# A 2x2 average pool on one core: the scheduler's straight-line program, and hand-written hardware loops with semaphores that are counted back down

## The chip, the cores and the metric

One NeuronCore of one Trainium2 chip. The metric is the device time of one execution in microseconds (us), on that core. A profile comes from one execution; its "span" is about 1.8 us shorter than the time reported for the same execution (3102.3 and 3104.08 in the profile of the kernel before).

## The reference

```python
def setup_inputs():
    return {'x': np.random.randn(32, 128, 256, 256).astype(np.float32), 'kernel_size': 2, 'stride': 2}

def reference(x, kernel_size, stride):            # cut to what matters
    for i in range(h_out):
        for j in range(w_out):
            window = x[:, :, 2*i:2*i + 2, 2*j:2*j + 2]
            output[:, :, i, j] = np.mean(window, axis=(2, 3))
    return output                                  # (32, 128, 128, 128) float32
```

1073.7 MB are read and 268.4 MB written, for three additions and one multiplication per output. Moving the data is what takes the time: the profile below has the DMA engines 90% or more busy in every slice.

## The kernel before

A row pair of the image (512 values) gives one output row (128 values). A tile is 32 row pairs on each of 128 partitions: 8 MB in, 2 MB out. There are 127 whole tiles, and a last one that is loaded in four parts of 16, 8, 4 and 4 row pairs, so that the work after the last byte is short.

```python
    in_pool = ctx.enter_context(tc.tile_pool(name="inp", bufs=2))
    out_pool = ctx.enter_context(tc.tile_pool(name="outp", bufs=4))

    def pool(it, dst):
        nc.vector.tensor_add(out=it[:, :, 0:w], in0=it[:, :, 0:w], in1=it[:, :, w:])     # L54
        nc.vector.tensor_add(out=dst, in0=it[:, :, 0:w:2], in1=it[:, :, 1:w:2])          # L55
        nc.scalar.mul(out=dst, in_=dst, mul=0.25)                                        # L56
    # ... cut: block() gives the rows of a tile in x and in out, tiles() a pair of buffers
    for k in range(whole):                       # 127 tiles
        xt, ot = block(k * TILE * P, TILE)
        it, res = tiles()
        nc.sync.dma_start(out=it, in_=xt)
        pool(it, res)
        if k < whole - 1:
            nc.scalar.dma_start(out=ot, in_=res)
        else:
            held = (ot, res)                     # stored later, from SyncE
    # ... cut: the last tile's four loads, the held store, then for each part:
        pool(it[:, a:b], res[:, a:b])
        nc.scalar.dma_start(out=ot, in_=res[:, a:b])
```

The Python loop is written out into the program: the trace has 392 instructions on VectorE, 397 on ScalarE and 270 on SyncE. The framework (Tile) places every wait.

Of the kernel before, what the change touches and what calls it, by code (L numbers as in the profile page):

```python
# [1 line left out]

# [4 lines left out]


@with_exitstack  # L10
def kernel(
    ctx: ExitStack,
    tc: tile.TileContext,
    x: bass.AP,
    kernel_size: bass.AP,
    stride: bass.AP,
    out: bass.AP,
):
    nc = tc.nc
    P = nc.NUM_PARTITIONS  # L20

    n, c, h, w = x.shape
    k = int(kernel_size)
    s = int(stride)
    h_out = (h - k) // s + 1
    w_out = (w - k) // s + 1
    R = n * c * h_out
    units = R // P if R % P == 0 else 0


    if k == 2 and s == 2 and h % 2 == 0 and w == 256 and units >= 1024:
        _pool_2x2(ctx, tc, x, out, units)
    else:
        _generic_pool(ctx, tc, x, out, k, s, n, c, h, w, h_out, w_out)


TILE = 32


def _pool_2x2(ctx, tc, x, out, units):  # L40
    nc = tc.nc
    P = nc.NUM_PARTITIONS
    f32 = mybir.dt.float32
    w = x.shape[3]
    w_out = w // 2

    xv = x.rearrange("n c (ho a) w -> (n c ho) (a w)", a=2)
    ov = out.rearrange("n c ho wo -> (n c ho) wo")

    in_pool = ctx.enter_context(tc.tile_pool(name="inp", bufs=2))  # L50
    out_pool = ctx.enter_context(tc.tile_pool(name="outp", bufs=4))

    def pool(it, dst):
        nc.vector.tensor_add(out=it[:, :, 0:w], in0=it[:, :, 0:w], in1=it[:, :, w:])  # L54
        nc.vector.tensor_add(out=dst, in0=it[:, :, 0:w:2], in1=it[:, :, 1:w:2])  # L55
        nc.scalar.mul(out=dst, in_=dst, mul=0.25)  # L56

    def block(r0, g):
        rows = slice(r0, r0 + g * P)
        xt = xv[rows].rearrange("(p g) f -> p g f", p=P)  # L60
        return xt, ov[rows].rearrange("(p g) f -> p g f", p=P)

    def tiles():
        it = in_pool.tile([P, TILE, 2 * w], f32, name="in_tile")
        return it, out_pool.tile([P, TILE, w_out], f32, name="res")



    whole, rest = divmod(units - 1, TILE)
    rest += 1  # L70
    for k in range(whole):
        xt, ot = block(k * TILE * P, TILE)
        it, res = tiles()
        nc.sync.dma_start(out=it, in_=xt)  # L74
        pool(it, res)
        if k < whole - 1:
            nc.scalar.dma_start(out=ot, in_=res)
        else:
            held = (ot, res)



    it, res = tiles()
    parts, a = [], 0
    while a < rest:
        b = rest if rest - a <= 4 else a + (rest - a) // 2
        xt, ot = block((whole * TILE + a) * P, b - a)
        nc.sync.dma_start(out=it[:, a:b], in_=xt)
        parts.append((ot, a, b))
        a = b  # L90
    nc.sync.dma_start(out=held[0], in_=held[1])
    for ot, a, b in parts:
        pool(it[:, a:b], res[:, a:b])
        nc.scalar.dma_start(out=ot, in_=res[:, a:b])


def _generic_pool(ctx, tc, x, out, k, s, n, c, h, w, h_out, w_out):
    nc = tc.nc
    P = nc.NUM_PARTITIONS

    planes = n * c
    xp = x.rearrange("n c h w -> (n c) h w")
    op = out.rearrange("n c ho wo -> (n c) ho wo")

    if h_out <= 0 or w_out <= 0 or planes == 0:
        return

    max_in_bytes_per_part = 48 * 1024

    def rows_for(bi):  # L110
        return (bi - 1) * s + k

    BI = 1
    while BI < h_out and rows_for(BI + 1) * w * 4 <= max_in_bytes_per_part:
        BI += 1

    inv = 1.0 / float(k * k)

    pool = ctx.enter_context(tc.tile_pool(name="gen", bufs=2))

    for p0 in range(0, planes, P):
        pn = min(P, planes - p0)
        for i0 in range(0, h_out, BI):
            bi = min(BI, h_out - i0)
            rows_needed = rows_for(bi)

            in_t = pool.tile([P, rows_for(BI), w], mybir.dt.float32, name="g_in")
            nc.sync.dma_start(
                out=in_t[:pn, :rows_needed, :],
                in_=xp[p0 : p0 + pn, i0 * s : i0 * s + rows_needed, :],  # L130
            )

            acc = pool.tile([P, BI, w_out], mybir.dt.float32, name="g_acc")
            first = True
            for di in range(k):
                for dj in range(k):
                    src = in_t[
                        :pn,
                        di : di + (bi - 1) * s + 1 : s,
                        dj : dj + (w_out - 1) * s + 1 : s,  # L140
                    ]
                    if first:
                        nc.vector.tensor_copy(out=acc[:pn, :bi, :], in_=src)
                        first = False
                    else:
                        nc.vector.tensor_add(
                            out=acc[:pn, :bi, :], in0=acc[:pn, :bi, :], in1=src
                        )

            nc.scalar.mul(out=acc[:pn, :bi, :], in_=acc[:pn, :bi, :], mul=inv)  # L150

            nc.scalar.dma_start(
                out=op[p0 : p0 + pn, i0 : i0 + bi, :], in_=acc[:pn, :bi, :]
            )


# [1 line left out]
_INS = ['x', 'kernel_size', 'stride']  # L158
_OUTS = [((32, 128, 128, 128), 'float32')]

_NUMBERS = {'kernel_size': 2, 'stride': 2}


# [26 lines left out]
```

## Time and profile before

3104.2 us, median of 3 runs (3104.09 to 3104.42).

| | kernel before |
|---|---|
| DMA engines busy | 90% or more in all 40 slices |
| moved | 1342.26 MB, 433 GB/s over the span |
| VectorE busy | 54% |
| ScalarE busy | 15% |
| period of a tile | 24.18 us, of which VectorE works 13.2 |

The page of the kernel before. First the busy time of an engine; then the DMA's busy tenths and GB/s in 40 equal slices; then the DMA queues with packets, MB and share of the 16 engines; then groups of instructions (busy us, mean ns, idle us before them and what ended it).

```profile
span 3102.3 us, 1081 instructions
...
DVE 1679.7 (54%) x262; ACT 464.8 (15%) x132; POOL 0.2 (0%) x4
...
DMA  9999999999999999999999999999999999999999
GB/s 418 437 439 425 437 439 424 438 438 425 438 437 425 439 436 426 439 434 428 440 433 429 439 432 431 438 431 433 437 428 437 437 428 436 437 428 436 437 428 410
...
q1 hardware_dynamic: 19008, 1075.85, 80.1%
q10 hardware_dynamic: 18720, 266.35, 20.1%
q14 instruction: 8, 0.07, 0.0%
...
L54 DVE TENSOR_TENSOR in_tile<-in_tile 128x8192 f32<-128x8192 f32 (+1 forms) x131 | 1113.0, 8496 | 1404.2 <-DMA in_tile<-in_x_dram 1404.2
...
L55 DVE TENSOR_TENSOR res<-in_tile 128x4096 f32<-128x4096 f32 (+1 forms) x131 | 567.0, 4328 | 11.8 <-DVE in_tile L54 0.5
```

The DMA engines hardly rest: they are 90% or more busy in every slice, and loads (q1, 80.1%) and stores (q10, 20.1%) together fill them, at 433 GB/s. VectorE waits 1404 us in all, for loads. The small queue q14, of the kind "instruction" on the page, has 8 packets.

VectorE's timeline of the kernel before (start us, us long, what, idle before and what ended it):

```profile
22.69 8.69 DVE L54 TENSOR_TENSOR in_tile<-in_tile 128x8192 f32<-128x8192 f32 x1 [22.69 <-DMA in_tile<-in_x_dram]
...
42.02 8.69 DVE L54 TENSOR_TENSOR in_tile<-in_tile 128x8192 f32<-128x8192 f32 x1 [6.18 <-DMA in_tile<-in_x_dram]
...
66.57 8.69 DVE L54 TENSOR_TENSOR in_tile<-in_tile 128x8192 f32<-128x8192 f32 x1 [11.40 <-DMA in_tile<-in_x_dram]
...
477.66 8.69 DVE L54 TENSOR_TENSOR in_tile<-in_tile 128x8192 f32<-128x8192 f32 x1 [10.98 <-DMA in_tile<-in_x_dram]
...
501.84 8.69 DVE L54 TENSOR_TENSOR in_tile<-in_tile 128x8192 f32<-128x8192 f32 x1 [10.97 <-DMA in_tile<-in_x_dram]
510.62 4.43 DVE L55 TENSOR_TENSOR res<-in_tile 128x4096 f32<-128x4096 f32 x1
526.44 8.69 DVE L54 TENSOR_TENSOR in_tile<-in_tile 128x8192 f32<-128x8192 f32 x1 [11.39 <-DMA in_tile<-in_x_dram]
...
550.83 8.69 DVE L54 TENSOR_TENSOR in_tile<-in_tile 128x8192 f32<-128x8192 f32 x1 [10.77 <-DMA in_tile<-in_x_dram]
...
3067.22 8.69 DVE L54 TENSOR_TENSOR in_tile<-in_tile 128x8192 f32<-128x8192 f32 x1 [10.96 <-DMA in_tile<-in_x_dram]
```

Subtract the starts. From the third tile on the period is 24.18 us (477.66 to 501.84), but from 501.84 to 526.44 it is 24.60 and then 24.39. The trace's packet records put 8-KB packets of q14 at 525.3 and 540.4 us, in just this stretch. The last line is the last full load.

The tail of the kernel before, from its timeline (four of the parts' instructions and the issue of the last store):

```profile
3081.76 4.42 DVE L54 TENSOR_TENSOR in_tile<-in_tile 128x4096 f32<-128x4096 f32 x1 [1.34 <-DMA in_tile<-in_x_dram]
...
3086.28 2.29 DVE L55 TENSOR_TENSOR res<-in_tile 128x2048 f32<-128x2048 f32 x1
...
3088.60 1.91 ACT L56 ACTIVATE res<-res 128x2048 f32<-128x2048 f32 x1 [4.53 <-DVE res L55]
...
3096.45 0.34 ACTq L94 DMA_DIRECT2D out_dram<-res  x1
```

From the first partial add to the issue of the last store: 3096.45 - 3081.76 = 14.69 us. The second add of a part starts 0.10 us after the first ends, and ScalarE starts 0.03 us after VectorE's result (3086.28 + 2.29 = 3088.57, then 3088.60).

### The profile page before, as it was taken

The page shows a single profiled execution, that of the slowest core. Times are in us where ns is not written, and L with a number is a line of the kernel's source. Part 1 is how long each engine was busy: PE and PEld are TensorE (multiplying, and loading weights), DVE is VectorE, ACT ScalarE, POOL GpSimd, SP SyncE. Part 2 cuts the span into 40 slices and gives each one's busy share as a digit, 9 for nine tenths or more (in the row PEclk, how much of TensorE's full clock was granted, in tenths as well). Part 3 has the DMA queues.
Part 4 walks back from the last instruction along what each step waited for, and adds up shares of the span by engine and source line. Part 5 has one row for each costly group of instructions (what it writes and reads, how often), then busy time and mean ns, then how long its engine had stood idle before and what let it go on. Part 6 is the DMA issues. An engine that isn't in the chain of part 4 may idle for free.

```text
span 3102.3 us, 1081 instructions
## 1 busy us (share of the span) xinstructions
DVE 1679.7 (54%) x262; ACT 464.8 (15%) x132; POOL 0.2 (0%) x4
## 2 busy tenths in 40 slices
DVE  4555555555555555555555555555555555555556
ACT  1111111111111111111111111111111111111111
POOL 0000000000000000000000000000000000000000
DMA  9999999999999999999999999999999999999999
GB/s 418 437 439 425 437 439 424 438 438 425 438 437 425 439 436 426 439 434 428 440 433 429 439 432 431 438 431 433 437 428 437 437 428 436 437 428 436 437 428 410
DMA packets 37736, 1342.26 MB, mean 433 GB/s; under 512 B 4192, under 2 KB 4192, under 8 KB 4576
## 3 DMA queue, kind: packets, MB, share of 16 engines
q1 hardware_dynamic: 19008, 1075.85, 80.1%
q10 hardware_dynamic: 18720, 266.35, 20.1%
q14 instruction: 8, 0.07, 0.0%
HBM read 1073.74 MB, written 268.44 MB: 433 GB/s over the span
## 4 chain that ended last, share of the span: by engine, by line
DMA 72%; DVE 27%; issue 0%; DVEq 0%; ACT 0%; SPq 0%
DMA in_tile<-in_x_dram 72%; DVE in_tile L54 18%; DVE res L55 9%; DVEq L55 0%; ACT res L56 0%; SPq L74 0%
## 5 line engine op out<-in xcount | busy, mean ns | idle before, releaser
L54 DVE TENSOR_TENSOR in_tile<-in_tile 128x8192 f32<-128x8192 f32 (+1 forms) x131 | 1113.0, 8496 | 1404.2 <-DMA in_tile<-in_x_dram 1404.2
L56 ACT ACTIVATE res<-res 128x4096 f32<-128x4096 f32 (+1 forms) x131 | 463.5, 3538 | 2630.9 <-DVE res L55 2630.9
L55 DVE TENSOR_TENSOR res<-in_tile 128x4096 f32<-128x4096 f32 (+1 forms) x131 | 567.0, 4328 | 11.8 <-DVE in_tile L54 0.5
L56 ACT ACT_TABLE_LOAD x1 | 1.3, 1283 | 0.7 <-PEq L171 0.7
L171 POOL MEMSET const-bfloat16-1.0<- 128x1 bf16 x1 | 0.1, 102 | 0.0
L171 POOL MEMSET const-uint8-127<- 128x1 uint8 x1 | 0.1, 101 | 0.0
L171 POOL MEMSET const-float32-0.0<- 128x1 f32 x1 | 0.1, 99 | 0.2 <-issue 0.2
L171 POOL MEMSET const-float32-1.0<- 128x1 f32 x1 | 0.1, 98 | 0.0
## 6 DMA issues: line engine op xcount, KB each, us to landing
out_dram<-res ACTq DMA_DIRECT2D x126, 2048.0 KB, 31.6
in_tile<-in_x_dram SPq DMA_DIRECT2D x1, 4096.0 KB, 25.5
in_tile<-in_x_dram SPq DMA_DIRECT2D x1, 2048.0 KB, 30.0
in_tile<-in_x_dram SPq DMA_DIRECT2D x2, 1024.0 KB, 33.0
out_dram<-res SPq DMA_DIRECT2D x1, 2048.0 KB, 13.6
in_tile<-in_x_dram SPq DMA_DIRECT2D x127, 35.1
out_dram<-res ACTq DMA_DIRECT2D x1, 1024.0 KB, 8.3
out_dram<-res ACTq DMA_DIRECT2D x1, 512.0 KB, 6.1
```

What stands on the lines that cost most here:

```text
L54: nc.vector.tensor_add(out=it[:, :, 0:w], in0=it[:, :, 0:w], in1=it[:, :, w:])
L55: nc.vector.tensor_add(out=dst, in0=it[:, :, 0:w:2], in1=it[:, :, 1:w:2])
L56: nc.scalar.mul(out=dst, in_=dst, mul=0.25)
L171: nc = _bacc.Bacc("TRN2", target_bir_lowering=False, num_devices=1)
```

## The change

The intent: take scheduling out of the framework's hands. One critical section holds the work; each engine runs a short hardware loop; each wait is followed by counting the same semaphore back down, so that a loop's body can wait on constants. The core of the diff (cut):

```diff
+    def take(engine, sem, n=1):
+        engine.wait_ge(sem, n)
+        engine.sem_inc(sem, -n)
+    def tile_load(t, b):
+        sp.dma_start(out=ins[b], in_=xt[t]).then_inc(loaded[b], 16)
+    def tile_sum(b, o, first=False):
+        it, dst = ins[b], res[o]
+        take(dve, loaded[b], 16)
+        dve.tensor_add(out=it[:, :, 0:w], in0=it[:, :, 0:w], in1=it[:, :, w:]).then_inc(ready)
+        if not first:
+            take(dve, stored[o], 16)
+        take(dve, ready)
+        dve.tensor_add(out=dst, in0=it[:, :, 0:w:2], in1=it[:, :, 1:w:2]).then_inc(summed)
+    def tile_scale(b, o, done):
+        take(act, summed)
+        act.sem_inc(free[b])
+        act.mul(out=res[o], in_=res[o], mul=0.25).then_inc(done)
+    def tile_store(t, o):
+        take(act, scaled)
+        act.dma_start(out=ot[t], in_=res[o]).then_inc(stored[o], 16)
...
-    for k in range(whole):
-        nc.sync.dma_start(out=it, in_=xt)
-        pool(it, res)
-        ...
+    with tc.tile_critical():
+        for b in range(2):
+            tile_load(b, b)
+        with sp.Fori(2, 2 + 2 * ((whole - 2) // 2), 2) as i:      # SyncE
+            for b in range(2):
+                take(sp, free[b])
+                tile_load(i + b, b)
...
+        for o in range(OUTS):                                     # VectorE: first four, then a loop
+            tile_sum(o % 2, o, first=True)
+        with dve.Fori(0, loops) as i:
+            for o in range(OUTS):
+                tile_sum(o % 2, o)
...
+        for t in range(OUTS):                                     # ScalarE: first four, then a loop
+            tile_scale(t % 2, t, scaled)
+            tile_store(t, t)
+        with act.Fori(OUTS, OUTS + loops * OUTS, OUTS) as i:
+            for o in range(OUTS):
+                tile_scale(o % 2, o, scaled)
+                tile_store(i + o, o)
...                                                               # cut: the parts, in the same style
+        take(sp, tail, 16 * len(parts))                           # SyncE waits for all stores
+        for o in range(OUTS):
+            if o != whole % OUTS:
+                take(sp, stored[o], 16)
```

A wait with its count-down becomes one separate semaphore instruction ahead of the work (386 of them on VectorE in the trace after, one for each `take` that it runs). In the loops, SyncE's loads and ScalarE's stores take their HBM address from a register (the same trace has 124 FUSED_REGOPS instructions on SyncE and 120 on ScalarE, as many as the loops issue loads and stores). The buffer is freed by ScalarE now, when it sees the sum, not by VectorE.

More of the change, by code (lines that the diff above doesn't have):

```diff
@@ L37 @@
 TILE = 32
+OUTS = 4
 def _pool_2x2(ctx, tc, x, out, units):
@@ L45, in _pool_2x2 @@
     w_out = w // 2
+    sp, act, dve = nc.sync, nc.scalar, nc.vector
     xv = x.rearrange("n c (ho a) w -> (n c ho) (a w)", a=2)
@@ L50, in _pool_2x2 @@
     in_pool = ctx.enter_context(tc.tile_pool(name="inp", bufs=2))
-    out_pool = ctx.enter_context(tc.tile_pool(name="outp", bufs=4))
-    def pool(it, dst):
-        nc.vector.tensor_add(out=it[:, :, 0:w], in0=it[:, :, 0:w], in1=it[:, :, w:])
-        nc.vector.tensor_add(out=dst, in0=it[:, :, 0:w:2], in1=it[:, :, 1:w:2])
-        nc.scalar.mul(out=dst, in_=dst, mul=0.25)
+    out_pool = ctx.enter_context(tc.tile_pool(name="outp", bufs=OUTS))
+    ins = [in_pool.tile([P, TILE, 2 * w], f32, name="in_tile") for _ in range(2)]
@@ new lines, in _pool_2x2 @@
+    res = [out_pool.tile([P, TILE, w_out], f32, name="res") for _ in range(OUTS)]
+    loaded = [ctx.enter_context(nc.semaphore(f"loaded{b}")) for b in range(2)]
+    free = [ctx.enter_context(nc.semaphore(f"free{b}")) for b in range(2)]
+    summed = ctx.enter_context(nc.semaphore("summed"))
+    scaled = ctx.enter_context(nc.semaphore("scaled"))
+    stored = [ctx.enter_context(nc.semaphore(f"stored{b}")) for b in range(OUTS)]
+    tail = ctx.enter_context(nc.semaphore("tail"))
+    ready = ctx.enter_context(nc.semaphore("ready"))
@@ L58, in block @@
+    held = ctx.enter_context(nc.semaphore("held"))
+    def take(engine, sem, n=1):
+        engine.wait_ge(sem, n)
+        engine.sem_inc(sem, -n)
     def block(r0, g):
         rows = slice(r0, r0 + g * P)
-        xt = xv[rows].rearrange("(p g) f -> p g f", p=P)
-        return xt, ov[rows].rearrange("(p g) f -> p g f", p=P)
-    def tiles():
-        it = in_pool.tile([P, TILE, 2 * w], f32, name="in_tile")
-        return it, out_pool.tile([P, TILE, w_out], f32, name="res")
+        return xv[rows].rearrange("(p g) f -> p g f", p=P), ov[rows].rearrange("(p g) f -> p g f", p=P)
@@ L69, in _pool_2x2 @@
     whole, rest = divmod(units - 1, TILE)
     rest += 1
-    for k in range(whole):
-        xt, ot = block(k * TILE * P, TILE)
-        it, res = tiles()
-        nc.sync.dma_start(out=it, in_=xt)
-        pool(it, res)
-        if k < whole - 1:
-            nc.scalar.dma_start(out=ot, in_=res)
-        else:
-            held = (ot, res)
-    it, res = tiles()
+    xt = xv[0:whole * TILE * P].rearrange("(t p g) f -> t p g f", p=P, g=TILE)
+    ot = ov[0:whole * TILE * P].rearrange("(t p g) f -> t p g f", p=P, g=TILE)
@@ new lines, in _pool_2x2 @@
+    loops, left = divmod(whole - OUTS, OUTS)
+    def tile_load(t, b):
[8 more added lines that the diff above has]
+        dve.tensor_add(out=dst, in0=it[:, :, 0:w:2], in1=it[:, :, 1:w:2]).then_inc(summed)
@@ L86, in _pool_2x2 @@
         b = rest if rest - a <= 4 else a + (rest - a) // 2
-        xt, ot = block((whole * TILE + a) * P, b - a)
-        nc.sync.dma_start(out=it[:, a:b], in_=xt)
-        parts.append((ot, a, b))
+        parts.append((a, b))
         a = b
-    nc.sync.dma_start(out=held[0], in_=held[1])
-    for ot, a, b in parts:
-        pool(it[:, a:b], res[:, a:b])
-        nc.scalar.dma_start(out=ot, in_=res[:, a:b])
+    psem = [ctx.enter_context(nc.semaphore(f"part{k}")) for k in range(len(parts))]
@@ new lines, in _pool_2x2 @@
+    with tc.tile_critical():
[5 more added lines that the diff above has]
+                tile_load(i + b, b)
+        t = 2 + 2 * ((whole - 2) // 2)
+        while t < whole:
+            take(sp, free[t % 2])
+            tile_load(t, t % 2)
+            t += 1
+        take(sp, free[whole % 2])
+        it, dst = ins[whole % 2], res[whole % OUTS]
+        for (a, b), s in zip(parts, psem):
+            sp.dma_start(out=it[:, a:b], in_=block((whole * TILE + a) * P, b - a)[0]).then_inc(s, 16)
+        take(sp, held)
+        sp.dma_start(out=ot[whole - 1], in_=res[(whole - 1) % OUTS]).then_inc(stored[(whole - 1) % OUTS], 16)
+        for o in range(OUTS):
[3 more added lines that the diff above has]
+                tile_sum(o % 2, o)
+        for o in range(left):
+            tile_sum(o % 2, o)
+        take(dve, stored[whole % OUTS], 16)
+        for (a, b), s in zip(parts, psem):
+            take(dve, s, 16)
+            dve.tensor_add(out=it[:, a:b, 0:w], in0=it[:, a:b, 0:w], in1=it[:, a:b, w:]).then_inc(ready)
+            take(dve, ready)
+            dve.tensor_add(out=dst[:, a:b], in0=it[:, a:b, 0:w:2], in1=it[:, a:b, 1:w:2]).then_inc(summed)
+        for t in range(OUTS):
[5 more added lines that the diff above has]
+                tile_store(i + o, o)
+        for t in range(OUTS + loops * OUTS, whole):
+            tile_scale(t % 2, t % OUTS, scaled if t < whole - 1 else held)
+            if t < whole - 1:
+                tile_store(t, t % OUTS)
+        act.sem_inc(free[(whole + 1) % 2], -1)
+        for a, b in parts:
+            take(act, summed)
+            act.mul(out=dst[:, a:b], in_=dst[:, a:b], mul=0.25).then_inc(scaled)
+            take(act, scaled)
+            act.dma_start(out=block((whole * TILE + a) * P, b - a)[1], in_=dst[:, a:b]).then_inc(tail, 16)
+        take(sp, tail, 16 * len(parts))
+        for o in range(OUTS):
+            if o != whole % OUTS:
+                take(sp, stored[o], 16)
```

## The prediction

> **What bounds it now.** The DMA engines. The page's slices show them 90% or more busy throughout, at 433 GB/s over the span (1342 MB in 3102.3 us); the two queues' shares add to 100%. [...] VectorE is busy 54%, ScalarE 15%. The timeline shows a tile every 24.18 us; VectorE works 13.2 us of it and idles 11.0 us, waiting for a load. A load takes 35.1 us to land because it stands behind the other buffer's load. So a buffer could come free up to about 11 us later before the load queue ran dry.
>
> **Steady state.** Same work, shapes and DMA rows (64 KB in, 16 KB out), two input and four output buffers. New per tile: separate semaphore instructions, freeing by way of ScalarE, a register-computed address before a DMA, a branch every two or four tiles. One semaphore instruction: before's first four tiles have none between the two adds and a gap of 0.04 us; later tiles have one and 0.09 us. So 0.05 us each; estimate for all of the above 0.3 to 1 us per tile, against 11 us of slack (VectorE, SyncE) and 20 us (ScalarE). Nothing of it is on the critical path: the period stays 24.18 us.
>
> **Gain.** Straight-line code is fetched during the run: the packet records put 8 packets of the instruction queue (8192 bytes, 309 ns each) inside the span, at 525, 540, 918, 1541, 1557, 2467, 2582 and 2598 us. The only tiles whose period exceeds 24.18 us by over 0.1 us, but for the third tile, lie at these fetches; their excess sums to 2.3 us. With loops (22 instructions on VectorE, 27 on ScalarE, 9 on SyncE) these vanish, save one or two near the end. [...]
>
> **Cost.** [...] Tail (from 3081.8 us, a critical chain of adds, scales and small stores): some five more semaphore instructions at 0.05 us, 0.3 us. [...]
>
> **Sum.** 3104.2 - 2.3 + 0.2 + 0.3 + 0.6 + 0.2 (a late fetch) = 3103.2 us. Range 3101.5 to 3107.0. Chances: faster by over 2% 0.01, within 2% 0.97, slower by over 2% 0.02.
>
> **Would show it right.** Period 24.18 us with hardly a longer tile; 433 to 434 GB/s; the instruction queue down from 8 packets to about 2 in the span; VectorE's idle time still about 11 us per tile, ended by loads; last load landing about 2 us earlier, then a tail about 1 us longer. Wrong if: dozens of instruction packets, or the last load no earlier.
>
> **Would make it wrong.** Back branches that fetch each time: some 120 packets of 0.31 us (loops run 62, 30 and 30 times); if they fall on one DMA engine, up to 40 us more. Register-addressed DMAs that are split otherwise, or cost several us to issue: then idle appears before loads. An exit handshake of several us.

Two terms of the sum: + 0.2 us for the start and + 0.6 us for the end; with these the sum came to 3103.2 us. No trace is named for either, nor for the + 0.2 us for a late fetch: the three are guesses, and without them the sum would be 3104.2 - 2.3 + 0.3 = 3102.2 us. That the loops' back branches would fetch nothing was not shown beforehand either; the result shows it.

## More of the kernel before

All runs told here are at a granted clock of 1.0. The experiments ran in four batches, on three chips (numbered 10 for e1 to e4 and e12, 5 for e5 to e8, 3 for e9 to e11), each with the kernel before beside them.

## The result, and the profile after

Ratios below are the mean time of one kernel's runs over that of the other's runs of the same rounds, so not quite the ratio of the medians quoted.

| | before | after |
|---|---|---|
| time, median (6 runs each) | 3104.14 us (3103.98 to 3104.54) | 3104.06 us (3103.83 to 3104.85) |
| ratio | | 1.0 (0.9987 to 1.0013) |
| instruction packets in the span | 8 | 2 |
| period of a tile | 24.18 us, six longer by over 0.1 us after the third tile | 24.18 us, none longer after the third tile |
| last full load seen by VectorE | 3067.22 us | 3067.18 us |

The page after, the same parts (less the lines that say nothing new):

```profile
span 3103.1 us, 2444 instructions
...
DMA  9999999999999999999999999999999999999999
...
q14 instruction: 2, 0.02, 0.0%
...
L88 DVE TENSOR_TENSOR in_tile<-in_tile 128x8192 f32<-128x8192 f32 x127 | 1104.0, 8693 | 1395.9 <-DVEq L70 1395.9
...
L92 DVE TENSOR_TENSOR res<-in_tile 128x4096 f32<-128x4096 f32 x127 | 562.0, 4425 | 18.6
```

A whole tile's first add takes 8693 ns, before 8692 (the group shown of before mixes in the parts, so its mean is lower), and the DMA is as full. The instruction queue is down to 2 packets. The releaser has changed its name: VectorE's idle time is now ended by "DVEq L70", its own sequencer's semaphore instruction. Nothing else is waited for: the wait for the load has moved from the add to that instruction.

VectorE's timeline after, the same stretches:

```profile
23.07 8.69 DVE L88 TENSOR_TENSOR in_tile<-in_tile 128x8192 f32<-128x8192 f32 x1 [23.07 <-DVEq L70]
...
42.42 8.69 DVE L88 TENSOR_TENSOR in_tile<-in_tile 128x8192 f32<-128x8192 f32 x1 [6.08 <-DVEq L70]
...
68.72 8.69 DVE L88 TENSOR_TENSOR in_tile<-in_tile 128x8192 f32<-128x8192 f32 x1 [13.04 <-DVEq L70]
...
479.80 8.69 DVE L88 TENSOR_TENSOR in_tile<-in_tile 128x8192 f32<-128x8192 f32 x1 [10.92 <-DVEq L70]
...
503.98 8.69 DVE L88 TENSOR_TENSOR in_tile<-in_tile 128x8192 f32<-128x8192 f32 x1 [10.92 <-DVEq L70]
512.82 4.43 DVE L92 TENSOR_TENSOR res<-in_tile 128x4096 f32<-128x4096 f32 x1
528.15 8.69 DVE L88 TENSOR_TENSOR in_tile<-in_tile 128x8192 f32<-128x8192 f32 x1 [10.91 <-DVEq L70]
...
552.35 8.69 DVE L88 TENSOR_TENSOR in_tile<-in_tile 128x8192 f32<-128x8192 f32 x1 [10.93 <-DVEq L70]
...
3067.18 8.69 DVE L88 TENSOR_TENSOR in_tile<-in_tile 128x8192 f32<-128x8192 f32 x1 [10.93 <-DVEq L70]
```

Around 504 to 552 us the periods are 24.18, 24.17 and 24.20 us: the two long tiles of before are gone. But look at the start. The third tile comes 68.72 - 42.42 = 26.30 us after the second; before, 24.55. The changed kernel is then 2.15 us late (68.72 against 66.57), of which 0.38 came from its start. What the fetches cost the kernel before later on, 2.3 us, brings the two level again. That is why VectorE sees the last full load at the same time in both (3067.22 and 3067.18 us). This profile is of the slowest of the six runs after (3104.85 us; the profiled run before took 3104.08 us, near its median), so a second one was needed (e1).

The tail after, the same instructions:

```profile
3081.73 4.42 DVE L145 TENSOR_TENSOR in_tile<-in_tile 128x4096 f32<-128x4096 f32 x1 [1.28 <-DVEq L70]
...
3086.30 2.29 DVE L147 TENSOR_TENSOR res<-in_tile 128x2048 f32<-128x2048 f32 x1
...
3088.71 1.91 ACT L164 ACTIVATE res<-res 128x2048 f32<-128x2048 f32 x1 [4.45 <-ACTq L70]
...
3096.97 0.34 ACTq L166 DMA_DIRECT2D out_dram<-res  x1
```

3096.97 - 3081.73 = 15.24 us, 0.55 more than before. A handover from VectorE to ScalarE takes 0.12 us (3086.30 + 2.29 = 3088.59, then 3088.71), before 0.03. The semaphore instructions themselves, by their line:

```profile
L70 DVEq EVENT_SEMAPHORE  x386: 21/21/21, 23.0 to 3095.3; - x193
L70 ACTq EVENT_SEMAPHORE  x261: 17/17/17, 36.4 to 3096.9; - x131
```

They last 21 ns on VectorE and 17 ns on ScalarE. Waiting in an instruction of its own, and only then handing out the work, costs more than those: 0.09 us at this handover, and between the two adds of a whole tile the gap went from 0.09 to 0.15 us (503.98 + 8.69 = 512.67, then 512.82). The number of semaphore instructions is not what counts there: the gap is 0.15 us in all 131 pairs of adds, whether one stands between them (the first four tiles and the parts) or two (all others). In the steady state nothing comes of it; VectorE has 10.9 us to spare.

**Reading a load by its 16 shares.** In the packet records every load of a whole tile has 128 packets of 64 KB and 16 completion packets of 4 bytes, and on average 16.0 packets are under way at once (before, from 1000 to 1001 us). I read a completion packet as the end of one DMA engine's share of the load. Here is when they came for five loads, in us after the first of the 16 (worked out from the records, sorted; only the last four of 16 shown):

```
           load 2               load 21              load 64              load 106             load 126
before     0.23 0.32 0.33 0.42  0.31 0.31 0.35 0.40  0.39 1.00 1.14 1.75  0.39 1.45 1.75 1.78  0.39 1.69 1.78 2.59
after      0.33 0.48 0.64 2.42  0.33 0.48 0.64 2.42  0.33 0.48 0.64 2.42  0.33 0.48 0.64 2.42  0.48 0.51 0.64 2.42
```

Thirteen engines of the kernel before stay within 0.4 us of each other for 3 ms; three fall behind in steps, and each step lies at a fetch packet (one of them also slips by about 0.4 us from load 39 to load 62, where there is no packet). The records do not name the engine of a packet: that a lag is one engine's is read from its staying the same from load to load. In the changed kernel's profile one engine is 2.42 us behind from load 2 on, and no share moves by more than 0.05 us after that until the fetch at 3040 us. The first share of load 126 comes at 3064.26 us before and at 3064.28 after. It is the last share that a load waits for: it came at 3066.86 us before and at 3066.71 after, and VectorE's add started at 3067.22 and 3067.18.

That is the theory (A): **a fetch packet sets back the one DMA engine it falls on, the setback stays because that engine has no idle time to catch up in, and a load lands with its slowest engine.** The rivals: (C) only the total work of the 16 engines counts, and eight packets of 309 ns are then nothing; and for the lag at the third tile, which took the gain away: that ScalarE's table load had moved from 0.7 us to 36.5 us into the stream (1), that it is an accident of single executions (2), or that it comes from the loops and their register-addressed loads (3).

### The profile page after: what moved, and what is told of

Same layout as the page of the kernel before. It is cut to its first block, busy times and chain, and to the rows that moved or that the text cites. A ratio compares the mean times of both kernels' runs of the same rounds, so it can differ in the third digit from the quotient of the medians.

```text
span 3103.1 us, 2444 instructions
## 1 busy us (share of the span) xinstructions
DVE 1679.7 (54%) x262; ACT 464.8 (15%) x132; POOL 0.2 (0%) x4
## 5 line engine op out<-in xcount | busy, mean ns | idle before, releaser
L88 DVE TENSOR_TENSOR in_tile<-in_tile 128x8192 f32<-128x8192 f32 x127 | 1104.0, 8693 | 1395.9 <-DVEq L70 1395.9
L97 ACT ACTIVATE res<-res 128x4096 f32<-128x4096 f32 x127 | 459.2, 3616 | 2587.2 <-ACTq L70 2587.2
L92 DVE TENSOR_TENSOR res<-in_tile 128x4096 f32<-128x4096 f32 x127 | 562.0, 4425 | 18.6
L145 DVE TENSOR_TENSOR in_tile<-in_tile 128x1024 f32<-128x1024 f32 (+2 forms) x4 | 9.1, 2287 | 1.3 <-DVEq L70 1.3
L97 ACT ACT_TABLE_LOAD x1 | 1.3, 1283 | 36.5 <-ACTq L70 36.5
```

The lines of the kernel that those rows point to most:

```text
L88: dve.tensor_add(out=it[:, :, 0:w], in0=it[:, :, 0:w], in1=it[:, :, w:]).then_inc(ready)
L92: dve.tensor_add(out=dst, in0=it[:, :, 0:w:2], in1=it[:, :, 1:w:2]).then_inc(summed)
L97: act.mul(out=res[o], in_=res[o], mul=0.25).then_inc(done)
L145: dve.tensor_add(out=it[:, a:b, 0:w], in0=it[:, a:b, 0:w], in1=it[:, a:b, w:]).then_inc(ready)
```

## The experiments

All gave correct results. What is read here is about 0.1%, from ranges of times that do not overlap (e3, e5, e9) and from the traces. "Lag" is the distance of the last of the 16 shares of a load from the first.

### e1: the changed kernel again

No edit.

> The changed kernel once more, unaltered, for a second profile. In the first one the third tile came 26.30 us after the second (before: 24.55), because one of the 16 DMA engines fell 1.75 us behind the rest, and kept that lag to the end; the first profile was also the slowest of its six runs (3104.85 against a median of 3104.06). Theory 1, the lag belongs to the change: third tile again at 26 us or more, the slowest share of a load 1.5 us or more behind the second slowest, 3104.1 us or more. Theory 2, the lag is an accident of one run: third tile at 24.5 us, spread of the 16 shares about 0.6 us, last full load landing at about 3065.2 us, about 3102.3 us by the clock of the run.

3103.90 us (3103.78 to 3104.06; before in the same rounds 3104.09). The third tile came 24.33 us after the second. VectorE's timeline of this run:

```profile
42.26 8.69 DVE L88 TENSOR_TENSOR in_tile<-in_tile 128x8192 f32<-128x8192 f32 x1 [6.06 <-DVEq L70]
...
66.59 8.69 DVE L88 TENSOR_TENSOR in_tile<-in_tile 128x8192 f32<-128x8192 f32 x1 [11.07 <-DVEq L70]
```

The lag at load 2 is 0.51 us, so it is no fixed part of the changed kernel (theory 2's number for the third tile). But the last full load was seen at 3065.98 us, not at 3065.2, and the gain in time is 0.2 us, not 1.8. The records show why: one engine drifted from 0.50 us behind at load 40 to 1.34 at load 126, with no step over 0.05 us from one load to the next, and the tail and the end are longer (table below).

### e2: the table loaded early

```diff
+        dve.memset(scratch, 0.0).then_inc(warm)          # VectorE, before its first tile
+        take(act, warm)                                  # ScalarE, before its first tile
+        act.mul(out=scratch, in_=scratch, mul=0.25)      # 128x1
```

> The changed kernel with one 128x1 activation on ScalarE before its loop, so that the activation table is loaded in the first 3 us as it was before the change, and not at 36.5 us, between the first sum and the first store. Theory 1 (the late table load, by delaying the first store past the end of the second load, is what set one DMA engine back): third tile at 24.5 us, no lagging engine, 3102.3 us. Theory 2 (accident): the same time as the unaltered changed kernel within 0.3 us. Theory 3 (loop entry or register-addressed loads): lag stays at about 1.75 us, time 3104 us.

3103.95 us (3103.78 to 3104.59). The table load came at 1.19 us, and still the third tile came 26.10 us after the second, with three engines 1.24, 1.49 and 2.23 us behind. Theory 1 is wrong.

### e3: the loops written out

```diff
-        with sp.Fori(2, 2 + 2 * ((whole - 2) // 2), 2) as i:
+        for i in range(2, 2 + 2 * ((whole - 2) // 2), 2):
-        with dve.Fori(0, loops) as i:
+        for i in range(loops):
-        with act.Fori(OUTS, OUTS + loops * OUTS, OUTS) as i:
+        for i in range(OUTS, OUTS + loops * OUTS, OUTS):
```

> The changed kernel with its three hardware loops written out: same semaphores, constant addresses, no branches. Theory A (what the change gains is instruction fetches that no longer take turns on the DMA engines): the instruction queue shows about 12 packets inside the span (five for ScalarE and five for VectorE, at 5 instructions a tile each, two for SyncE); each sets its engine back by 0.5 to 0.85 us as in before, so ScalarE's five cost about 4 us at the slowest engine; last full load lands at about 3069 us and the time is 3106 to 3108 us. Theory B (fetches do not matter): 3104 us, last load at 3067 us. If the lag at the third tile is due to loops it is absent here.

3106.78 us (3106.61 to 3106.87), 2.7 us more than before. Its page:

```profile
span 3104.9 us, 1613 instructions
...
q14 instruction: 12, 0.10, 0.0%
```

VectorE's first add of the last full load, from its timeline:

```profile
3069.07 8.69 DVE L88 TENSOR_TENSOR in_tile<-in_tile 128x8192 f32<-128x8192 f32 x1 [10.91 <-DVEq L70]
```

Twelve packets, as counted from the program. They come in two series 25.7 tiles apart (322.8 and 943.3 us, for example: 620.5 / 24.18), which at five instructions a tile is 128 instructions, and in a third at 909.3 and 2457.7 us, 64 tiles of SyncE's two instructions, again 128. The last full load was seen at 3069.07 us (expected 3069); the lag there is 4.30 us, and the steps of the slowest engine are 0.85 us each at loads 64 and 116 and 0.84 at load 90. Against e1, which differs by the loops alone and has the same tail and end (table below), it is 2.9 us slower for ten packets more. Theory C is refuted: 0.08 MB more on 16 engines is 0.2 us at 433 GB/s.

### e4: the kernel before, with a late table load

```diff
-        nc.scalar.mul(out=dst, in_=dst, mul=0.25)
+        if late:                                         # tile 0 alone
+            nc.vector.tensor_scalar_mul(out=dst, in0=dst, scalar1=0.25)
+        else:
+            nc.scalar.mul(out=dst, in_=dst, mul=0.25)
```

> The kernel before, with the first tile scaled by VectorE [...] so that ScalarE first issues a store and then loads its table, at about 38 to 40 us, in the stream. Nothing else altered. If the late table load by itself, or through what it delays, sets a DMA engine back: third tile 26 us, 3105.9 us. If not: 3104.1 us within 0.4.

3104.13 us (3104.06 to 3104.44). The table load fell at 38.57 us, the third tile came after 24.64 us, lag 0.50 us. A late table load costs nothing here, which agrees with e2.

### e5: more code to fetch, on an engine that does nothing

```diff
     with tc.tile_critical():
+        for _ in range(640):
+            nc.gpsimd.sem_inc(idle, 1)
+            nc.gpsimd.sem_inc(idle, -1)
```

> The changed kernel with 1280 semaphore instructions (plus one, minus one, on a semaphore that nobody waits for) on GpSimd, which otherwise does nothing: more code to fetch, nothing else. Theory A (a fetch packet sets back the one DMA engine that it falls on, by 0.55 to 0.85 us as the packets of before did, and a load lands when its slowest engine is done, so only the largest sum on one engine counts): about 10 more packets on the instruction queue in the first 150 us, all of GpSimd's on one DMA engine; the 16 shares of a load then differ by 5.5 to 8.5 us for the rest of the run, and the time is 3108.5 to 3111.5 us. Theory C (only the total work of the 16 engines counts): 10 packets of 0.31 us over 16 engines are 0.2 us, and the time is 3104.1 us.

3108.38 us (four runs 3108.11 to 3108.76, a fifth 3113.68, for which no profile exists). Its page and VectorE's timeline:

```profile
span 3107.0 us, 3727 instructions
...
q14 instruction: 12, 0.10, 0.0%
```

```profile
44.95 8.69 DVE L89 TENSOR_TENSOR in_tile<-in_tile 128x8192 f32<-128x8192 f32 x1 [7.39 <-DVEq L71]
...
70.65 8.69 DVE L89 TENSOR_TENSOR in_tile<-in_tile 128x8192 f32<-128x8192 f32 x1 [12.43 <-DVEq L71]
...
96.80 8.69 DVE L89 TENSOR_TENSOR in_tile<-in_tile 128x8192 f32<-128x8192 f32 x1 [12.89 <-DVEq L71]
...
121.64 8.69 DVE L89 TENSOR_TENSOR in_tile<-in_tile 128x8192 f32<-128x8192 f32 x1 [11.57 <-DVEq L71]
...
145.80 8.69 DVE L89 TENSOR_TENSOR in_tile<-in_tile 128x8192 f32<-128x8192 f32 x1 [10.90 <-DVEq L71]
```

Ten packets came between 10.4 and 102.2 us, one every 10 us: ten for 1280 instructions, again one per 128. The periods of these tiles are 25.70, 26.15, 24.84 and then 24.16 us: it slows while the packets come, and it never gets the time back. The lag is 6.96 us from load 6 to load 126, all of it on one engine; the other fifteen are within 1.1 us. So all ten packets must have gone to the same DMA engine, at about 0.64 us each ((6.96 - 0.6) / 10, with 0.6 us as the lag that load 2 has without them). The time is 0.1 us under the expected range, its mechanism as expected by theory A; C expected 3104.1. GpSimd's instructions touch nothing that the other engines wait for, and e3, which adds nothing on GpSimd, shows such steps at its packets too: fetching is what the two have in common.

### e6: ScalarE's loop from tile 0

```diff
-        for t in range(OUTS):
-            tile_scale(t % 2, t, scaled)
-            tile_store(t, t)
-        with act.Fori(OUTS, OUTS + loops * OUTS, OUTS) as i:
+        with act.Fori(0, OUTS + loops * OUTS, OUTS) as i:   # and the early table load of e2
```

> The changed kernel with ScalarE's loop begun at tile 0 (no four tiles written out ahead of it, 17 instructions fewer before the end, table loaded early by a 128x1 activation). ScalarE's one fetch of the changed kernel, at 3040 us, ahead of the last full load, should move past the last load or disappear. Where no engine lags at the third tile, the last full load then lands at about 3065.4 us (second profile of the changed kernel: 3065.98) and the time is 3103.4 us; if the late fetch costs nothing, 3103.9 us.

3104.22 us (3103.83 to 3104.61). The fetch at 3040 us did move, to 3088.9; the last full load was seen at 3066.23 us with a lag of 1.57, no earlier than in e1. A miss: the late fetch had fallen on an engine that was not the slowest, so it had cost nothing. Here too the slowest engine drifted, from 0.64 us at load 20 to 1.57.

### e7: the tail's waits on the instructions themselves

From e6.

```diff
-            take(dve, s, 16)
+            dve.wait_ge(s, 16)          # folded into the add; counted down once, at the end
...
-            take(act, summed)
+            act.wait_ge(tsum, k + 1)    # likewise for ready and scaled
```

> The same, and in the last, partial tile every wait is put on the instruction that needs it, on semaphores of its own that are counted down once at the end, instead of a separate wait-and-count-down before each. If that separate instruction is what lengthens the tail (from the first partial add to the last store's issue 15.2 us in the changed kernel, 14.7 in before), the tail is back at 14.7 us and the time is 0.5 us under that of the run with ScalarE's loop begun at tile 0, about 3102.9 us. If it is not, the two times agree within 0.2 us.

3104.06 us (3103.41 to 3104.75). The tail of this run:

```profile
3081.28 4.43 DVE L149 TENSOR_TENSOR in_tile<-in_tile 128x4096 f32<-128x4096 f32 x1 [1.17 <-DMA in_tile<-in_x_dram]
...
3085.74 2.29 DVE L151 TENSOR_TENSOR res<-in_tile 128x2048 f32<-128x2048 f32 x1
...
3088.07 1.91 ACT L170 ACTIVATE res<-res 128x2048 f32<-128x2048 f32 x1 [4.14 <-DVE res L151]
...
3095.91 0.34 ACTq L172 DMA_DIRECT2D out_dram<-res  x1
```

3095.91 - 3081.28 = 14.63 us, and the handover to ScalarE is back at 0.04 us: the separate wait is what had lengthened the tail. The time does not show it, 3104.06 us where 3102.9 was expected: in the profiled execution two engines were late at load 2 (1.03 and 2.18 us), and the five times spread over 1.3 us.

### e8: the kernel before again

> The kernel before, unaltered, for a second profile: is the lag of one DMA engine at the third tile (seen in the first profile of the changed kernel and with the early table, not in the changed kernel's second profile, not with loops written out) possible in this kernel as well? If it is an accident of an execution, it may show here (third tile over 25 us) in some executions; if it belongs to register-addressed loads, never. The eight fetch packets lie within 20 us of those of the first profile, and the largest lag at the last full load is again 2.3 to 2.9 us.

3104.22 us (3104.02 to 3104.65). The eight packets lie within 0.6 us of those of the first profile. Third tile after 24.60 us, lag 0.94 at load 2 and 3.07 at the last full load (a little over the expected 2.3 to 2.9), with the slowest engine stepping by about 0.84 us at each of the loads 22, 64 and 107; at load 38 the first share, which the lag is counted from, itself came 0.39 us later. No jump at load 2.

### e9: only SyncE's loop written out

From e7, SyncE's loop as a Python loop, as in e3.

> The run with ScalarE's loop from tile 0 and the tail's waits on its instructions, with SyncE's loop alone written out: constant load addresses, loops kept on VectorE and ScalarE. So far one DMA engine fell 1.6 us or more behind at the third load in three of six profiles of kernels with a register-addressed third load, and in none of four with constant addresses. Theory R (the first register-addressed load is what can set a DMA engine back): third tile 24.3 to 24.6 us, SyncE's two fetches add about 1.3 us to one engine, largest lag at the last full load 1.6 to 2.0 us, and the five times lie within 0.5 us of each other (they spread over 1.3 us in the run with all three loops). Theory S (accident, or the loops of the other engines): a lag of over 1.6 us at the third load is possible here as well, and the times spread over 1 us or more.

3105.22 us (3104.71 to 3105.55). No engine was late at load 2 (0.68 us; third tile after 24.66), but the times spread over 0.8 us and the lag at the last full load is 2.62, more than either theory said: the engine that drifts (0.82 us at load 39, 1.82 at load 100) first stands out at load 37, at SyncE's first packet, and steps up at SyncE's second (2.54 at load 101), so drift and packets add up.

### e10 and e11: the first register-addressed load moved to load 6

```diff
+        for j in range(2, 6):
+            take(sp, free[j % 2])
+            tile_load(j, j % 2)
-        with sp.Fori(2, 2 + 2 * ((whole - 2) // 2), 2) as i:
+        with sp.Fori(6, 2 + 2 * ((whole - 2) // 2), 2) as i:
```

> The changed kernel with SyncE's loads 2 to 5 written out with constant addresses, so that load 6 is the first register-addressed one. Theory R: no engine lags at load 2 (third tile 24.3 to 24.6 us); if one falls behind by 1 us or more, it is at load 6. Theory S: a lag, if there is one, is at load 2, when the first store starts. No lag at all leaves it open.

> The same kernel again, for a second profile, because the lag comes in about half of the executions. Theory R: none at load 2, possibly one at load 6. Theory S: at load 2 or not at all.

3104.08 and 3104.14 us (two runs each). No lag at load 2 (0.34 and 0.55 us), and none at load 6. This leaves it open.

### e12: all of it together

e7 with loads 2 to 5 on constant addresses.

> The run with ScalarE's loop from tile 0 and the tail's waits on its instructions, with loads 2 to 5 on constant addresses as in the two runs whose third tile had no lag. If the late third tile is what hid the shorter tail in that run, the largest lag at the last full load is 1.3 to 1.6 us, first partial add to last store's issue 14.6 us, and the time is 3103.5 us (3103.3 to 3103.7), 0.6 us under before; if the lag turns up here, 3104 us and a spread of over 1 us.

3104.01 us (3103.76 to 3104.31; before in the same rounds 3104.18): a miss by 0.5 us, though everything that was to be mended was mended. Lag 1.33 us, last full load seen at 3066.14, tail 14.63 us. The profiles' stages, in us:

| run | lag, load 126 | last full load seen | first partial add to last store's issue | issue to last DMA packet's end | from there to the end of the span | span |
|---|---|---|---|---|---|---|
| before | 2.59 | 3067.22 | 14.69 | 4.58 | 1.27 | 3102.3 |
| e8, before again | 3.07 | 3067.80 | 14.68 | 4.59 | 1.27 | 3102.9 |
| after | 2.42 | 3067.18 | 15.24 | 4.52 | 1.58 | 3103.1 |
| e1, after again | 1.34 | 3065.98 | 15.25 | 4.54 | 1.72 | 3102.0 |
| e3, loops written out | 4.30 | 3069.07 | 15.24 | 4.46 | 1.62 | 3104.9 |
| e7, tail's waits | 2.18 | 3066.85 | 14.63 | 4.62 | 1.61 | 3102.1 |
| e12, together | 1.33 | 3066.14 | 14.63 | 5.28 | 1.72 | 3102.2 |

In e12 the last store is issued at 3095.18 us, 1.27 us earlier than before, and takes 0.7 us longer to land; against e7 it is issued 0.73 us earlier and the last packet ends only 0.07 us earlier (3100.53, then 3100.46). The packet records say why. This is the mean number of busy DMA engines in each of the last microseconds (packets overlap a little in the records, so it can come out over 16):

```
us of the span    3097  3098  3099  3100
before            16.6  11.1   3.1   1.4
e1, after again   16.5  16.1   2.8   0.3
e12, together     16.4  16.8   5.5   0.5
```

Before, engines begin to run out of work between 3098 and 3099 us, while the slowest has yet to finish. In e12 they are all busy until 3099, with stores that were still to be written, and the last small store stands behind them. From these counts I estimate that the work of the 16 engines, evenly shared, would end at about 3099.0, 3099.2 and 3099.5 us in the three, against 3101.03 us for the last packet of before: at most 2 us could be had from all this. No version found here is faster than the kernel before by more than the spread of its runs.

## Why the prediction was right or wrong

The range (3101.5 to 3107.0) held the time, and "within 2%" came true. Neither says much for the reasoning: all the terms together come to 1 us of 3104, so "within 2%" could hardly fail, and the range is wide enough for any of the runs here but e5. The measured difference, 0.08 us, is within the noise. The point, 3103.2 us, was 0.9 us too low, and of the prediction's own tests one, "Wrong if: ... the last load no earlier", went against it in the first profile. Term by term:

- **The bound and the steady state: right.** The period is 24.18 us in both, the DMA as full, VectorE idle 10.9 us per tile. Freeing by ScalarE, register addresses and branches cost nothing there.
- **Fetches vanish: right, and shown.** 8 packets became 2. That they matter to a kernel bound by DMA is shown by e3 (12 packets, 3106.78 us) and e5 (10 more packets, 3108.38 us). The back branches fetched nothing: the two packets after came at 3040 and 3091 us, behind the loops' last branch (3012.4 us), and none in their 122 turns. What the prediction did not see is the form of the cost: three of the eight packets fell on the engine that ended up slowest, 0.8 us each; the others fell on engines that had time to spare. A packet's setback, about 0.64 us in e5 and up to 0.85 us at the steps in e3 and e8, is two to three times its own 309 ns. VectorE itself loses next to nothing: the only such gap in its trace before is 0.50 us instead of 0.09 between two adds at 535 us, 5 us ahead of a packet, against 10.8 us of idle time that follow.
- **"- 2.3": this is the step that failed, in size.** "last load landing about 2 us earlier" measured 0.04 us earlier in the changed kernel's first profile, and 1.24 in its second. Taking the fetches away does not make the 16 engines even. In some executions one or more falls behind at the third load (2.2 to 2.4 us of lag: after, e2, e7), and then no engine drifts; in the others (e1, e6, e10 to e12) one drifts to 1.3 to 1.6 us over the run. Either takes the place of much of what the fetches had cost.
- **"+ 0.2" for the start: about right.** The first load was issued at 0.96 us, before at 0.73; VectorE saw it 0.25 to 0.38 us later.
- **"+ 0.3" for the tail: too small.** 0.55 us. The count, five more waits in the chain, was right; the size of one was not. The 0.05 us came from semaphore instructions that had little to wait for; one that holds the chain up costs 0.06 to 0.11 us between two adds (0.39 us over the four parts, from gaps of 0.09, 0.03, 0.03 and 0.03 us to 0.15 each), 0.09 us at the last handover to ScalarE and 0.07 us before the issue of the last store. e7 shows the cause by taking these waits away.
- **"+ 0.6" for the end: too large.** From the last packet to the end it is 0.3 to 0.45 us more (table above).
- **"+ 0.2" for a late fetch: not found.** The fetch at 3040 us fell on an engine that was not the slowest (e6).

So the gain of the fetches was real, was lost again, wholly or in part, to lags that the changed kernel shows of itself, and what was left paid for a tail and an end that were 0.9 us longer.

What stays open: what sets an engine back at load 2. It came in three of six profiles in which load 2 had a register address (after, e2, e7; not e1, e5, e6), and in none of eight in which it had a constant one. That points to the first register-addressed load, but three of six against none of eight may still be chance, three of the eight (e9 to e11) ran on chip 3, where no experiment had a register-addressed load 2, and in e10, e11 and e12 it did not show at load 6. Nor is it known what makes one engine drift, in both kernels (before: about 0.4 us from load 39 to load 62; e10: from 0.34 to 1.46 us over the run).

## What to carry to other kernels

When the DMA engines have no idle time, ask not how much work a change takes off them but which one of the 16 it takes it off: a load lands with its slowest engine (before, load 126: first share at 3064.26 us, last at 3066.86, VectorE's add at 3067.22), and a setback of one engine stays until the end (e5: 6.96 us from load 6 to load 126). Code that is fetched during such a stream is a load on one DMA engine (here 0.64 us a packet in e5, up to 0.85 us in e3): hand-placed waits without loops, at five instructions a tile on VectorE and on ScalarE, cost 2.9 us of 3104 (e3 against e1), and loops take that away, but no more than that. Before mending a tail, look whether the queues behind it are already empty; if they are not, a store issued earlier lands hardly earlier (e12 against e7: 0.73 us at the issue, 0.07 us at the last packet).
